# A Hymba block on one core: half blocks of matmuls between the transposes of the norm stretch, two more tiles' first products there, and the last phase's first loads and splits issued early

## The chip, the cores and the metric

The kernel runs on one core of a Trainium2 chip. The metric is the time of one execution on the device in microseconds (us). Five engines run their own instruction streams and wait for each other by semaphores: TensorE (PE in the rows), VectorE (DVE), ScalarE (ACT), GpSimd (POOL) and SyncE (SP), which here issues all DMAs.

## What is computed

One decoder block over 1,024 tokens (and 16 meta tokens), width 1,024, feed-forward width 2,816, everything in float32. The part that matters here:

```python
h = h + rms_norm(mix @ w_out, ln_post_mix)       # post_norm
hn = rms_norm(h, ln_pre_ffn)                     # second_norm
gu = hn @ w_gate_up
ff = (silu(gu[..., :D_FF]) * gu[..., D_FF:]) @ w_down
h = h + rms_norm(ff, ln_post_ffn)
```

## The kernel before

A float32 product runs as three matmuls on a high and a low part of each operand (high·high, high·low, low·high). The high part is a rounding copy (ACT, a CAST row), the low part the difference (DVE); the code calls making them a split. Times below are those of the profiled execution.

**Attention and projections** end at about 525 us. The change leaves the order of all engines there as it is.

**The norm stretch** (525 to 617 us). For each of the eight row tiles (128 tokens) the rest of the out-projection is added to `y` (half blocks `pz`, 12 matmuls each, `half_out`), `post_norm` scales it (a factor `ry` made by ACT and POOL, a gain multiply `y<-y,gpost` on POOL, the residual add on DVE), `second_norm` multiplies by the second norm's factor `rh` and the gain `gfb` (one DVE instruction), and the result is transposed on TensorE through `ident` into a PSUM tile (`tz`, `tzt`; two buffers) from which ACT and DVE split it into the operands `b11`, `b21` (tiles 0 to 3), `b22` and the sums `bt1` to `bt4` (tiles 4 to 7). The sums' inputs `c` come from `combine_rows` (three POOL and one DVE instruction per tile).

**The main loop** (617 to 1025 us) takes 22 tiles of the feed-forward width. Each is a Strassen–Winograd scheme of seven products of 12 matmuls (128x512) with DVE, ACT and POOL work beside. Products 1 and 2 of a tile ("11"·b11 and "12"·b21) need only the first half of the norms, so `blocks` runs those of the first `N_AHEAD` = 3 tiles inside the stretch, into PSUM banks `q`. The other operands of a tile are sums of weight blocks: `combos` (four POOL instructions `cw`), each then split into `as`. After each product `after` reads its bank: an ACT copy (`s<-q`, `p<-q`), a DVE add, a Silu on ACT. Every second tile POOL forms activation sums (`store_acts`, four instructions `s<-s`) and, but for the last, sums of down-projection weights (`store_down`, four `rd`), which SP stores to DRAM (`act`, `down`).

**The last phase** (1025 to about 1243 us) is the down projection in 77 steps of 12 matmuls. Each step loads one `act` block and one weight block back (`rab`), splits both into `hl`, and multiplies into eight banks (`px`, `py`). The splits of the last 11 steps are made ahead, from step 33 on, one in every three steps.

**Order.** PE, ACT, DVE and POOL are pinned to the order in which the code issues their instructions up to the end of the main loop; SP and the last phase are ordered by a scheduler. In the code before, that scheduler also moved loads and splits of the last phase's first steps up into the last tiles of the main loop.

Of the kernel before, what the change touches and what calls it, by code (L numbers as in the profile page):

```python
# [21 lines left out]
P = 128  # L22
# [75 lines left out]
def hymba_kernel(ctx, tc, x, meta, rel_bias, g_pre_mix, g_post_mix, g_pre_ffn, g_post_ffn,  # L98
# [4 lines left out]
    class Pinned:  # L103
# [49 lines left out]
    ident = cp.tile([P, P], F32, name="ident")  # L153
    make_identity(nc, ident)
# [3 lines left out]
    bfb = cp.tile([P, 8], F32, name="bfb")  # L158
    mix71 = cp.tile([P, 2, 512], F32R, name="mix71")
    pool.memset(cp.tile([P, PAD_LEFT], F32, name="pad_left"), 0.0)  # L160
# [798 lines left out]
    def down(dst, acts, ws_, t, half):  # L959
# [3 lines left out]
        for i, ((ah, al), (wh, wl)) in enumerate(zip(acts, ws_)):  # L963
            pe.matmul(dst, ah[:, ts_], wh[:, hs], start=i == 0, stop=False)
            pe.matmul(dst, ah[:, ts_], wl[:, hs], start=False, stop=False)
            pe.matmul(dst, al[:, ts_], wh[:, hs], start=False, stop=i == n - 1)

# [174 lines left out]
    t3l = h2p.tile([P, 4, HALF], F32R, name="bt3l")  # L1142
    bp, b_st = open_pool("bst", "left")
    psB_st = ExitStack()
    psB = psB_st.enter_context(tc.tile_pool(name="psB", bufs=1, space=PSUM, reuse_waits="tile"))

    def half_out(t, half):
        g = psB.tile([P, 512], F32, name=f"pz{t}{half}", tag="G", bufs=6)
        down(g, mh, wos_b, t - 4, half)
        ys = y_of[t][:, half * 512:half * 512 + 512]  # L1150
        return lambda: dve.tensor_tensor(ys, g, ys, op=ALU.add)
# [7 lines left out]

    gfb = bp.tile([P, D], F32, name="gfb")  # L1160
    sp.dma_start(gfb, g_pre_ffn[0].partition_broadcast(P))
# [8 lines left out]
    def combine_rows(t):  # L1170
# [3 lines left out]
        pool.tensor_tensor(t3, b22, b12, op=ALU.subtract)  # L1174
        pool.tensor_tensor(t1, b12, b11, op=ALU.subtract)
        pool.tensor_tensor(t2, t3, b11, op=ALU.add)
        rows_of[t] = dict(zip(("t3", "t1", "t2", "t4"), c))
        return lambda: dve.tensor_tensor(t4, b21, t2, op=ALU.subtract)
# [3 lines left out]
    def transposes(src, n, t):  # L1182
# [4 lines left out]
        split(tp, b_op[n][0][:, :, cs], b_op[n][1][:, :, cs])  # L1187


    op_homes = iter("gggg" + "ww" + "wwggg" + "oooog" + "wwwwo" + ("ggggooo" + "wwwwooo") * NF)  # L1190

    def op_tile(name):
        home = next(op_homes)
        pl, tag = (gup, "gu") if home == "g" else (ws, "whl") if home == "w" else (opp, "op")
# [50 lines left out]
    def product(dst, f_, an, bn, fresh, last):  # L1245
        (bh, bl), a = b_op[bn], a_op.pop((f_, an))
        for k in range(4):
# [357 lines left out]
```

## Time and profile before

| what | value |
|---|---|
| runs | 1254.54, 1255.61, 1252.38 us; median 1254.54 |
| the profiled execution's own time, and its span | 1251.34 us, 1249.5 us |
| mean granted clock of TensorE in it | 0.972 |
| TensorE busy | 1174.8 us (94% of the span) |
| DVE, ACT, POOL busy | 775.5, 554.2, 524.9 us |
| out-projection ends, norm stretch | 525 to 617.10 us |
| main loop, 148 products | 617.10 to 1025.42 us |

A profile row gives the start, the duration, the engine, the operation, out<-in by the program's names, how many instructions run together (x), and in brackets how long the engine had been idle just before and which engine's result ended that. The granted clock is 1.00 at 2.4 GHz and 0.50 at 1.2 GHz; a value between is a mixture over the slice.

### The profile page before, as it was taken

The numbers are of one execution on the slowest core, as the hardware profiler recorded it, in microseconds if no ns is written. First come the engines' busy times: TensorE is split into PE (matmuls) and PEld (weight loads), VectorE is DVE, ScalarE is ACT, GpSimd is POOL, SyncE is SP. The second block draws the span as 40 slices with busy tenths as digits, with TensorE's granted clock in tenths as the row PEclk, the third lists the DMA queues.
The fourth block names the chain that finished last, engine by engine and source line by source line (L and its number), as shares of the span: only waits on it lengthen the run. The fifth ranks groups of instructions, "written<-read, shape, count | busy, mean of one in ns | idle before, by whom it ended". The sixth has DMA issues, their size and how long they took to land.

```text
span 1249.5 us, 17350 instructions
## 1 busy us (share of the span) xinstructions
PE 1174.8 (94%) x5967; PEld 997.5 (80%) x5967; DVE 775.5 (62%) x1625; ACT 554.2 (44%) x1178; POOL 524.9 (42%) x529
## 2 busy tenths in 40 slices
PE   7989999999999899876799999999999999999997
PEld 6978889988988787764688888888888777888876
DVE  6477776656666777576566555555556634446764
ACT  5366565555554543342533333333333324445541
POOL 7243234343433333376357557665567630000001
PEclk9999999999999999977899999999999999999999
DMA  7521123131311512532235455435455358666745
GB/s 225 155 76 41 38 66 99 44 92 45 91 44 45 155 44 76 184 119 67 68 104 193 150 177 177 156 132 166 146 186 182 133 202 266 186 198 223 252 154 200
DMA packets 133383, 167.31 MB, mean 134 GB/s; under 512 B 10612, under 2 KB 82292, under 8 KB 133294
## 3 DMA queue, kind: packets, MB, share of 16 engines
q1 hardware_dynamic: 133294, 166.20, 41.8%
q8 instruction: 47, 0.77, 0.3%
q14 instruction: 42, 0.34, 0.1%
HBM read 114.17 MB, written 46.56 MB: 129 GB/s over the span
## 4 chain that ended last, share of the span: by engine, by line
PE 72%; DVE 8%; POOL 6%; DMA 5%; issue 5%; ACT 3%; SPq 0%; POOLq 0%; DVEq 0%; ACTq 0%
PE q L113 30%; PE px L113 7%; PE py L113 5%; PE pvb L113 3%; PE pk L113 3%; PE pqb L113 3%; PE of L113 3%; PE pqa L113 2%; PE sf L113 2%; DMA rab<-act 2%; PE tf L113 2%; PE pyb L113 2%; PE pya L113 1%; PE o L113 1%; DVE hl L113 1%
## 5 line engine op out<-in xcount | busy, mean ns | idle before, releaser
L113 DVE TENSOR_TENSOR hl<-rab,hl 128x512 fp32r<-128x512 f32 x154 | 101.8, 707 | 84.3 <-ACT hl L113 84.0
L113 DVE TENSOR_TENSOR as<-cw,as 128x512 fp32r<-128x512 f32 x88 | 89.1, 1014 | 72.5 <-ACT as L113 71.7
L113 ACT CAST hl<-rab 128x512 fp32r<-128x512 f32 x154 | 87.9, 619 | 91.1 <-DMA rab<-act 37.2
L113 PE MATMUL px<-hl,hl 128*128 128x512 f32 x528 | 122.2, 393 | 2.7 <-ACT hl L113 2.7
L113 PEld LDWEIGHTS px<-hl,hl 128*128 128x128 f32 x528 | 100.0, 190 | 24.3 <-ACT hl L113 3.1
L113 PE MATMUL py<-hl,hl 128*128 128x512 f32 x396 | 90.5, 389 | 2.6 <-DVE hl L113 2.6
L113 PEld LDWEIGHTS py<-hl,hl 128*128 128x128 f32 x396 | 74.2, 188 | 18.4 <-DVE hl L113 3.0
L113 POOL TENSOR_TENSOR s<-s,s 128x512 f32<-128x512 f32 x44 | 69.3, 1596 | 32.1 <-DVE s L113 31.2
L113 POOL TENSOR_TENSOR cw<-wgu 128x512 f32<-128x512 f32 x22 | 29.9, 1359 | 124.0 <-DMA wgu<-in_w_gate_up_dram 85.3
L113 POOL TENSOR_SCALAR PF<-PF,lf 128x144 f32<-128x144 f32 (+3 forms) x64 | 51.4, 804 | 63.9 <-DVE lf L113 48.1
L113 POOL TENSOR_SCALAR rf0v<-sa 128x1 f32<-128x1 f32 x1 | 0.6, 562 | 180.8 <-DVE sa L113 180.8
L113 ACT ACTIVATE s<-s 128x512 f32<-128x512 f32 x44 | 27.8, 632 | 109.4 <-DVE s L113 109.4
L113 DVE TENSOR_TENSOR s<-q,s 128x512 f32<-128x512 f32 x66 | 45.5, 689 | 44.1 <-PE q L113 40.3
L113 ACT ACTIVATE PF<-PF,nf 128x144 f32<-128x144 f32 (+3 forms) x64 | 50.5, 790 | 47.2 <-DVE nf L113 46.4
L113 POOL TENSOR_TENSOR rd<-rd 128x512 f32<-128x512 f32 x44 | 65.4, 1486 | 12.3 <-DMA h<-h_dram 9.7
L113 ACT COPY s<-q 128x512 f32<-128x512 f32 x44 | 25.9, 588 | 95.6 <-PE q L113 65.5
L113 DVE TENSOR_TENSOR a<-wgg,a 128x512 fp32r<-128x512 f32 x44 | 47.7, 1089 | 31.7 <-ACT a L113 31.7
L113 PE MATMUL q<-b11h,a 128*128 128x512 f32 x176 | 62.2, 416 | 3.1 <-ACT b11h L113 3.1
L113 ACT CAST as<-cw 128x512 fp32r<-128x512 f32 x88 | 54.2, 618 | 20.8 <-PE q L113 15.8
L113 PE MATMUL q<-bt4h,a 128*128 128x512 f32 x176 | 59.1, 397 | 3.8 <-DVE p L113 3.8
L113 POOL TENSOR_SCALAR P<-P,ls 128x272 f32<-128x272 f32 (+1 forms) x64 | 29.6, 483 | 77.1 <-DVE ls L113 63.2
L113 PE MATMUL q<-b21h,a 128*128 128x512 f32 x176 | 60.9, 408 | 0.0
(468 smaller groups left out, 3407.4 us busy)
## 6 DMA issues: line engine op xcount, KB each, us to landing
act<-s SPq DMA_DIRECT2D x77, 256.0 KB, 3.7
rab<-act SPq DMA_DIRECT2D x77, 256.0 KB, 2.9
wgg<-in_w_gate_up_dram SPq DMA_DIRECT2D x25, 512.0 KB, 4.3
wgu<-in_w_gate_up_dram SPq DMA_DIRECT2D x22, 512.0 KB, 3.9
rd<-in_w_down_dram SPq DMA_DIRECT2D x11, 1024.0 KB, 4.9
down<-rd SPq DMA_DIRECT2D x44, 256.0 KB, 2.2
rab<-down SPq DMA_DIRECT2D x44, 256.0 KB, 3.6
wi<-in_w_in_dram SPq DMA_DIRECT2D x18, 512.0 KB, 3.7
```

The source lines that it names most:

```text
L113: i = fn(*a, **k)
```

## The change

The diff, cut to what changes the order of work or adds to it:

```diff
+            if i % 2 and i < n - 1:
+                yield
...
+    snp, snap_st = open_pool("snap", "left")
     bp, b_st = open_pool("bst", "left")
+    gfb = bp.tile([P, D], F32, name="gfb")
+    sp.dma_start(gfb, g_pre_ffn[0].partition_broadcast(P))
...
-        down(g, mh, wos_b, t - 4, half)
+        yield from down_parts(g, mh, wos_b, t - 4, half)
...
-    gfb = bp.tile([P, D], F32, name="gfb")
-    sp.dma_start(gfb, g_pre_ffn[0].partition_broadcast(P))
...
-        split(tp, b_op[n][0][:, :, cs], b_op[n][1][:, :, cs])
...
+        hi, lo = [x[:, :, cs] for x in b_op[n]]
+        act.copy(hi, tp)
+        between()
+        dve.tensor_tensor(lo, tp, f(hi), op=ALU.subtract)
...
-    N_AHEAD = 3
+
+    N_AHEAD, SNAP = 5, (3, 4)
+    p1_of, early_of = {}, {}
+
+    def first_products(f_):
+        for i, (an, bn) in ((1, ("11", "11")), (3, ("12", "21"))):
+            banks[f_, i] = b = bank(f"q{i}_{f_}")
+            for part in range(2):
+                product(b, f_, an, bn, True, i == 3, part)
+                if part == 0:
+                    yield None
+            if f_ not in SNAP:
+                yield lambda: None
+            elif i == 1:
+                both = snp.tile([P, 2, HALF], F32, name=f"early{f_}")
+                p1_of[f_], early_of[f_] = both[:, 0], both[:, 1]
+                yield lambda f_=f_, b=b: act.copy(p1_of[f_], b)
+            else:
+                yield lambda f_=f_, b=b: dve.tensor_tensor(early_of[f_], b, p1_of[f_], op=ALU.add)
...
-                yield half_out(t, half)
-        for f_ in range(N_AHEAD):
-            for i, (an, bn) in ((1, ("11", "11")), (3, ("12", "21"))):
-                banks[f_, i] = bank(f"q{i}_{f_}")
-                product(banks[f_, i], f_, an, bn, True, i == 3)
-                yield lambda: None
+                yield from half_out(t, half)
+        for f_ in SNAP + tuple(f_ for f_ in range(N_AHEAD) if f_ not in SNAP):
+            yield from first_products(f_)
 
     work = blocks()
-    add = [lambda: None]
-
-    def unit():
-
-        last = add[0]
-        add[0] = next(work, None) or (lambda: None)
-        return last
+    follow = []
+
+    def unit(n=1):
+
+        for _ in range(n):
+            got = next(work, None)
+            for x in follow:
+                x()
+            follow[:] = [got] if got else []
...
-    preps = {0: prepare_gate(0, act), 1: prepare_gate(1, act)}
-    for n in range(10):
-        if 1 <= n < 7:
+    preps = {0: 3, 1: 4, 4: 0, 5: 1, 6: 2}
+    for n in range(4):
+        gate = prepare_gate(preps[n], act) if n in preps else None
+        if n:
             square_sum(n + 1, "rh", junk[0])
-        first = unit() if n < 4 else None
-        if n < NT:
-            second_norm(n)
-        if first:
-            first()
-        if 5 <= n < 9:
-            fourth = combine_rows(n - 1)
+        unit(2)
+        second_norm(n)
+        if n:
+            transposes(halves(n - 1)[0], "11", n - 1)
+        unit()
+        if n:
+            transposes(halves(n - 1)[1], "21", n - 1)
+        unit()
+        post_norm(n + 2)
+        first_sum(n + 3)
+        if gate:
+            run(gate)
...
         if n >= 6:
-            transposes(rows_of[n - 2]["t3"], "t3", n - 2)
-            transposes(rows_of[n - 2]["t1"], "t1", n - 2)
-        if 1 <= n < 5:
-            transposes(halves(n - 1)[0], "11", n - 1)
-            transposes(halves(n - 1)[1], "21", n - 1)
-        elif 5 <= n < 9:
+            late = rows_of[n - 2]
+            transposes(late["t3"], "t3", n - 2, third[n - 2])
+        if n < NT:
+            second_norm(n)
+        if 5 <= n < 9:
+            first, second, third[n - 1] = combine_rows(n - 1)
+            first()
+        if n == 4:
+            transposes(halves(3)[0], "11", 3)
+        unit()
+        if n >= 6:
+            transposes(late["t1"], "t1", n - 2, (lambda: post_norm(n + 2)) if n + 2 < NT else lambda: None)
+        elif n == 5:
+            transposes(halves(4)[1], "22", 4, lambda: post_norm(7))
+        else:
+            post_norm(6)
+        unit()
+        if n == 4:
+            transposes(halves(3)[1], "21", 3)
+        elif 6 <= n < 9:
             transposes(halves(n - 1)[1], "22", n - 1)
-        if n < 9:
-            second = unit()
-        if n + 2 < NT:
-            post_norm(n + 2)
-        second()
-        second = lambda: None
-        if n >= 6:
-            transposes(rows_of[n - 2]["t2"], "t2", n - 2)
-            transposes(rows_of[n - 2]["t4"], "t4", n - 2)
         first_sum(n + 3)
         if 5 <= n < 9:
-            fourth()
-        if n in preps:
-            run(preps[n])
-        if n == 2:
-            for c in combos(0, bp, 2):
-                c()
-        elif n == 3:
-            preps[4] = prepare_gate(2, act)
-        elif n == 7:
-            split_block(0, "s1")
-        elif n == 8:
-            split_block(0, "s2")
-            split_block(0, "s4")
-    run(work)
-    for n in ("s3", "22"):
-        split_block(0, n)
+            second()
+        unit()
+        if n >= 6:
+            transposes(late["t2"], "t2", n - 2)
+        if n >= 7:
+            unit()
+        if n >= 6:
+            transposes(late["t4"], "t4", n - 2)
+        if gate:
+            run(gate)
+    unit(20)
...
+    pending = combos(0, fp, 2)
...
+        def read(to, b):
+            if p1 is None:
+                act.copy(to, b)
+            else:
+                dve.tensor_tensor(to, b, p1, op=ALU.add)
...
-            act.copy(p5_of[f_], b2)
+            read(p5_of[f_], b2)
...
-            act.copy(s_tile(f_, 1), b1)
+            read(s_tile(f_, 1), b1)
...
+            if p1 is not None:
+                dve.tensor_tensor(p1, b1, p1, op=ALU.add)
+            dve.tensor_tensor(s_of[f_, 0], b1 if p1 is None else p1, s_of[f_, 0], op=ALU.mult)
...
+        if n == 6 and f_ in SNAP:
+            banks[f_, 1], fresh = bank(f"q4_{f_}"), True
...
     held = None
+    names = ("s1", "s2", "s4", "s3", "22")
+    first, second = pending
+    first()
+    split_block(0, "s1")
+    second()
+    for n in names[1:]:
+        split_block(0, n)
     for f_ in range(N_AHEAD):
-        after(f_, 1)
-        after(f_, 2)
+        if f_ in SNAP:
+            s_of[f_, 0] = early_of[f_]
+            act.activation(early_of[f_], early_of[f_], AF.Silu)
+        else:
+            after(f_, 1)
+            after(f_, 2)
...
-        steps = []
+        parts = [lambda: [load(n) for n in range(3)]] + [lambda: None] + [lambda n=n: split_step(n) for n in range(3)]
...
-    sp.dma_start(gpost2, g_post_ffn[0].partition_broadcast(P))
...
-                load_h1(t)
+                if t == 3:
+                    load_h1(t)
...
     LOAD, SPLIT = 6, 3
-    done_load = done_split = 0
+    done_load = done_split = 3
...
-        if steps[n][0] >= 3 and n % 3 == 0 and early < len(steps):
+        if n == 4:
+            sp.dma_start(gpost2, g_post_ffn[0].partition_broadcast(P))
+        if n in (7, 18, 29):
+            load_h1((n - 7) // 11)
+        if n >= NP and n % 5 == 0 and early < len(steps):
             load(early)
             split_step(early)
             early += 1
```

In words: `down` and `product` can now run in two halves of six matmuls, and `unit()` sets one half (or one block) between two transposes. `N_AHEAD` is 5; tiles 3 and 4 go first, their first two products are copied (ACT) and added (DVE) into SBUF (`early`), and later reads add that part (DVE) where an ACT copy stood; product 6 of these tiles gets a bank of its own, `q4`. The gain `gfb` is loaded ahead of the rows `xt`. `combos(0)` and all splits of tile 0's sums come after the last transpose. Not shown: operand tiles get other buffers (`mix71` serves as one of them), the sums in `store_acts` have two buffers instead of four and each is stored as soon as it is made, and the last phase's step list, `load` and `split_step` move up unchanged but for which of two buffers they take.

Three places in the order of the engines. First TensorE in the middle of the stretch, before: `q1_1` is the first product of tile 1, `tz` and `tzt` are sets of four transposes, `c2_4` the second sum of row tile 4.

```order
L113 MATMUL q1_1_6941<-b11h_6542,a11_1_6678 128x512
L113 MATMUL tzt24_6954<-ident_63,c2_4_6871 128x128 x4
L113 MATMUL tzt44_6961<-ident_63,c4_4_6872 128x128 x4
L113 MATMUL tzt35_6977<-ident_63,c3_5_6906 128x128 x4
L113 MATMUL tzt15_6984<-ident_63,c1_5_6907 128x128 x4
L113 MATMUL tz226_6991<-ident_63,y6_5343 128x128 x4
L113 MATMUL q3_1_6998<-b21h_6544,a12_1_6681 128x512
```

After, where the first product of tile 0 stands at this place:

```order
L113 MATMUL q1_0_6975<-b11l_6543,a11_0_6858 128x512
L113 MATMUL q1_0_6975<-b11h_6542,a11_0_6858 128x512
L113 MATMUL tzt24_6983<-ident_70,c2_4_6875 128x128 x4
L113 MATMUL tzt44_6990<-ident_70,c4_4_6876 128x128 x4
L113 MATMUL tzt35_7003<-ident_70,c3_5_6940 128x128 x4
L113 MATMUL q1_0_6975<-b11h_6542,a11_0_6858 128x512
L113 MATMUL q1_0_6975<-b11l_6543,a11_0_6858 128x512
L113 MATMUL q1_0_6975<-b11h_6542,a11_0_6858 128x512 x2
L113 MATMUL q1_0_6975<-b11l_6543,a11_0_6858 128x512
L113 MATMUL q1_0_6975<-b11h_6542,a11_0_6858 128x512
L113 MATMUL tzt15_7024<-ident_70,c1_5_6941 128x128 x4
```

A product now stands in two halves with transposes between; six sets of transposes had stood almost back to back.

Second, the end of the stretch. On POOL the four `cw0` rows of `combos(0)` stood inside the stretch before, ahead of the factors of row tiles 4 and 6:

```order
L113 TENSOR_TENSOR y5_5342<-y5_5342,gpost_5905 128x1024
L113 TENSOR_TENSOR cw00_6746<-wgu0_6744 128x512
L113 TENSOR_TENSOR cw00_6746<-cw00_6746,wgg0_6742 128x512
L113 TENSOR_TENSOR cw01_6747<-wgg0_6742,wgu0_6744 128x512
L113 TENSOR_TENSOR cw01_6747<-wgg0_6742,cw00_6746 128x512
L113 TENSOR_SCALAR rh4v_6754<-srh4_6752 128x1
L113 TENSOR_TENSOR rh4r_6755<-rh4v_6754,mhalf_68 128x1
```

After, they stand behind the last sums of row tile 7:

```order
L113 TENSOR_TENSOR c2_6_7014<-c3_6_7012,y2_5339 128x512
L113 TENSOR_TENSOR c3_7_7081<-y7_5344 128x512
L113 TENSOR_TENSOR c1_7_7082<-y7_5344,y3_5340 128x512
L113 TENSOR_TENSOR c2_7_7083<-c3_7_7081,y3_5340 128x512
L113 TENSOR_TENSOR cw00_7199<-wgu0_7197 128x512
L113 TENSOR_TENSOR cw00_7199<-cw00_7199,wgg0_7195 128x512
L113 TENSOR_TENSOR cw01_7200<-wgg0_7195,wgu0_7197 128x512
```

On ACT, before, from the splits of the last transposes on (`a22_0` is tile 0's last weight block, `s00` its first read of a bank):

```order
L113 CAST bt2h_6913<-tzt27_7105 128x4x128
L113 CAST bt4h_6915<-tzt47_7112 128x4x128
L113 CAST as3_0_7132<-cw01_6747 128x512
L113 CAST a22_0_7135<-wgu0_6744 128x512
L113 COPY s00_7146<-q1_0_6833 128x512
L113 ACT_TABLE_LOAD
L113 ACTIVATE s00_7146<-s00_7146 128x512
L113 COPY s10_7150<-q1_1_6941 128x512
L113 ACTIVATE s10_7150<-s10_7150 128x512
L113 COPY s20_7154<-q1_2_7057 128x512
L113 ACTIVATE s20_7154<-s20_7154 128x512
L113 CAST as1_1_7179<-cw10_7162 128x512
```

After, from the same splits of tile 0's sums on:

```order
L113 CAST as3_0_7217<-cw01_7200 128x512
L113 CAST a22_0_7220<-wgu0_7197 128x512
L113 COPY s00_7223<-q1_0_6975 128x512
L113 ACT_TABLE_LOAD
L113 ACTIVATE s00_7223<-s00_7223 128x512
L113 COPY s10_7227<-q1_1_7059 128x512
L113 ACTIVATE s10_7227<-s10_7227 128x512
L113 COPY s20_7231<-q1_2_7128 128x512
L113 ACTIVATE s20_7231<-s20_7231 128x512
L113 ACTIVATE early3_6835<-early3_6835 128x512
L113 ACTIVATE early4_6909<-early4_6909 128x512
L113 CAST as1_1_7258<-cw10_7241 128x512
```

All splits of tile 0's sums moved behind the last transposes (`as1_0`, `as2_0`, `as4_0` stand in the three rows above this piece), and two activations of `early` are new ahead of `as1_1`.

Third, DVE in the last tile but one of the main loop. Before, with the splits `hl` of the last phase's first steps in it:

```order
L113 TENSOR_TENSOR a11_21_9922<-wgg21_9901,a11_21_9922 128x512
L113 TENSOR_TENSOR as1_21_9942<-cw210_9905,as1_21_9942 128x512
L113 TENSOR_TENSOR hl00_10238<-rab0_10217,hl00_10238 128x512
L113 TENSOR_TENSOR as2_21_9959<-cw210_9905,as2_21_9959 128x512
L113 TENSOR_TENSOR hl01_10241<-rab0_10217,hl01_10241 128x512
L113 TENSOR_TENSOR a12_21_9977<-wgg21_9901,a12_21_9977 128x512
L113 TENSOR_TENSOR s200_9925<-q3_20_9964,s200_9925 128x512
L113 TENSOR_TENSOR as3_21_9994<-cw211_9906,as3_21_9994 128x512
L113 TENSOR_TENSOR hl10_10244<-rab1_10220,hl10_10244 128x512
L113 TENSOR_TENSOR p5_20_9945<-q1_20_9907,p5_20_9945 128x512
L113 TENSOR_TENSOR as4_21_10010<-cw211_9906,as4_21_10010 128x512
L113 TENSOR_TENSOR hl11_10247<-rab1_10220,hl11_10247 128x512
```

After, the splits come behind tile 20's last multiplications:

```order
L113 TENSOR_TENSOR as2_21_9948<-cw210_9894,as2_21_9948 128x512
L113 TENSOR_TENSOR a12_21_9966<-wgg21_9890,a12_21_9966 128x512
L113 TENSOR_TENSOR s200_9914<-q3_20_9953,s200_9914 128x512
L113 TENSOR_TENSOR mix71_69<-cw211_9895,mix71_69 128x512
L113 TENSOR_TENSOR p5_20_9934<-q1_20_9896,p5_20_9934 128x512
L113 TENSOR_TENSOR as4_21_9998<-cw211_9895,as4_21_9998 128x512
L113 TENSOR_TENSOR s201_9951<-q2_20_9916,s201_9951 128x512
L113 TENSOR_TENSOR a22_21_10015<-wgu21_9892,a22_21_10015 128x512
L113 TENSOR_TENSOR s200_9914<-q1_20_9896,s200_9914 128x512
L113 TENSOR_TENSOR s201_9951<-p5_20_9934,s201_9951 128x512
L113 TENSOR_TENSOR hl00_10095<-rab0_10057,hl00_10095 128x512
L113 TENSOR_TENSOR hl01_10098<-rab0_10057,hl01_10098 128x512
```

`p5_20`, which empties the bank of tile 20's product 7, no longer stands behind `hl10`.

## Rows read from the trace of the kernel before

**Rows 1.** The page's first part: busy time of each engine, share of the span.

```profile
PE 1174.8 (94%) x5967; PEld 997.5 (80%) x5967; DVE 775.5 (62%) x1625; ACT 554.2 (44%) x1178; POOL 524.9 (42%) x529
```

**Rows 2.** Windows: PE, PEld, DVE, ACT, POOL busy; granted clock; DMA share, GB/s.

```profile
525.00:550.00 25.00, 20.05 (x89) 16.41 (x88) 19.72 (x23) 10.41 (x19) 16.72 (x14) 0.86 0.56 201
550.00:575.00 25.00, 12.91 (x48) 9.51 (x47) 15.10 (x13) 7.96 (x16) 22.90 (x20) 0.73 0.30 101
575.00:600.00 25.00, 16.06 (x67) 12.27 (x65) 13.32 (x16) 6.77 (x12) 14.14 (x12) 0.72 0.09 25
...
625.00:650.00 25.00, 25.00 (x112) 20.68 (x111) 15.25 (x18) 8.22 (x16) 11.37 (x8) 1.00 0.29 93
```

**Rows 3.** Timeline of PE in the norm stretch and at the main loop's start.

```profile
531.62 1.97 PE L113 MATMUL tz<-ident,y 128*128 128x128 f32 x8 [4.95 <-DVE y L113]
...
555.01 0.80 PE L113 MATMUL q<-b11h,a 128*128 128x512 f32 x1 [3.06 <-ACT b11h L113]
559.70 0.79 PE L113 MATMUL q<-b11l,a 128*128 128x512 f32 x1 [3.90 <-DVE b11l L113]
...
564.56 0.81 PE L113 MATMUL tz<-ident,y 128*128 128x128 f32 x4
...
572.17 1.11 PE L113 MATMUL tzt<-ident,c 128*128 128x128 f32 x4 [4.04 <-POOL c L113]
...
617.10 0.40 PE L113 MATMUL q<-bt1h,as 128*128 128x512 f32 x1
...
619.86 0.39 PE L113 MATMUL q<-bt2h,as 128*128 128x512 f32 x1
```

**Rows 4.** Timeline of SP's queue: the load of the second norm's gain.

```profile
523.30 0.48 SPq L1161 DMA_DIRECT2D gfb<-in_ln_pre_ffn_dram  x1
```

**Rows 5.** Timeline of DVE: second norms of row tiles 0 and 2.

```profile
530.28 1.28 DVE L113 SCALAR_TENSOR_TENSOR y<-y,rh0r,gfb 128x1024 f32<-128x1024 f32 x1 [9.45 <-DMA gfb<-in_ln_pre_ffn_dram]
...
540.47 3.41 DVE L113 SCALAR_TENSOR_TENSOR y<-y,rh2r,gfb 128x1024 f32<-128x1024 f32 x1
```

**Rows 6.** Timeline of POOL: gains of row tiles 2, 4 and 6, `combos(0)`, first sum of tile 4.

```profile
523.59 2.40 POOL L113 TENSOR_TENSOR y<-y,gpost 128x1024 f32<-128x1024 f32 x1
...
539.40 3.40 POOL L113 TENSOR_TENSOR y<-y,gpost 128x1024 f32<-128x1024 f32 x1
...
550.89 1.27 POOL L113 TENSOR_TENSOR cw<-wgu 128x512 f32<-128x512 f32 x1
...
555.55 1.27 POOL L113 TENSOR_TENSOR cw<-wgg,cw 128x512 f32<-128x512 f32 x1
...
559.70 2.37 POOL L113 TENSOR_TENSOR y<-y,gpost 128x1024 f32<-128x1024 f32 x1
...
570.86 1.26 POOL L113 TENSOR_TENSOR c<-y 128x512 f32<-128x512 f32 x1
```

**Rows 7.** Timeline of ACT where the norm stretch ends.

```profile
613.97 0.62 ACT L113 CAST a<-wgu 128x512 fp32r<-128x512 f32 x1
614.49 0.59 ACT L113 COPY s<-q 128x512 f32<-128x512 f32 x1
...
621.16 0.58 ACT L113 COPY p<-q 128x512 f32<-128x512 f32 x1
```

**Rows 8.** Timeline of POOL: sums of the first two tiles' activations, then of weights.

```profile
648.62 6.78 POOL L113 TENSOR_TENSOR s<-s,s 128x512 f32<-128x512 f32 x4 [3.87 <-DVE s L113]
655.36 6.40 POOL L113 TENSOR_TENSOR rd<-rd 128x512 f32<-128x512 f32 x4
```

**Rows 9.** Timeline of PE: the waits from the last tile on.

```profile
1001.95 0.79 PE L113 MATMUL q<-bt4h,a 128*128 128x512 f32 x1 [3.79 <-DVE p L113]
...
1006.36 0.39 PE L113 MATMUL q<-b11h,a 128*128 128x512 f32 x1
...
1036.45 23.44 PE L113 MATMUL px<-hl,hl 128*128 128x512 f32 x96 [2.70 <-ACT hl L113]
...
1190.80 21.84 PE L113 MATMUL py<-hl,hl 128*128 128x512 f32 x95 [2.61 <-DVE hl L113]
```

More of the change, by code (lines that the diff above doesn't have):

```diff
@@ L957, in load_rows, with down_parts @@
         return hi, lo
-    def down(dst, acts, ws_, t, half):
+    def down_parts(dst, acts, ws_, t, half):
         n = len(acts)
@@ L1243, in split_block, with product @@
         split_op(f_, n, blocks_of[f_][n])
-    def product(dst, f_, an, bn, fresh, last):
-        (bh, bl), a = b_op[bn], a_op.pop((f_, an))
-        for k in range(4):
+    def product(dst, f_, an, bn, fresh, last, part=None):
+        (bh, bl), a = b_op[bn], a_op[f_, an]
+        for k in range(4) if part is None else range(2 * part, 2 * part + 2):
             pe.matmul(dst, a[:, 0, k], bh[:, k], start=fresh and k == 0, stop=False, skip_group_check=True)
@@ L1381, in combined @@
     def combined(name, tag, op, a, b):
-        r = fp.tile([P, HALF], F32, name=name, tag=tag, bufs=4)
+        r = fp.tile([P, HALF], F32, name=name, tag=tag, bufs=2)
         pool.tensor_tensor(r, a, b, op=op)
@@ L1491, in split_step @@
             parts_of[n].append(hl)
+    held = None
+    names = ("s1", "s2", "s4", "s3", "22")
[5 more added lines that the diff above has]
+        split_block(0, n)
+    for f_ in range(N_AHEAD):
+        if f_ in SNAP:
[4 more added lines that the diff above has]
+            after(f_, 2)
+    pending = combos(1, fp, 2)
+    for f_ in range(NF):
+        ahead = f_ < N_AHEAD
+        order = (5, 6, 3, 7, 4) if ahead else (1, 5, 6, 2, 7, 3, 4)
+        names = ("s1", "s2", "s4", "s3", "22") if f_ + 1 < N_AHEAD else ("11", "s1", "s2", "12", "s3", "s4", "22")
+        parts = [lambda: [load(n) for n in range(3)]] + [lambda: None] + [lambda n=n: split_step(n) for n in range(3)]
+        if f_ + 1 < NF:
+            first, second = pending
+            parts = [lambda n=n: split_block(f_ + 1, n) for n in names]
+            if len(order) < len(names):
+                s2, s3 = parts[1:3], parts[3:5]
+                parts = [parts[0], lambda: [c() for c in s2], lambda: [c() for c in s3]] + parts[5:]
+            s0, s1 = parts[0:2]
+            parts[0] = lambda: (first(), s0())
+            parts[1] = lambda: (second(), s1())
+        parts = iter(parts)
+        for i, n in enumerate(order):
+            if n == 4 and ahead:
+                held = f_
+                next(parts, lambda: None)()
+                continue
+            multiply(f_, n, next(parts, lambda: None))
+            if i == 0 and held is not None and held != f_:
+                multiply(held, 4)
+                held = None
+        if f_ + 2 < NF:
+            pending = combos(f_ + 2, fp, 2)
+        j = f_ - 1
+        if j > 0 and j % 2:
+            store_acts(j // 2)
+            store_down(j // 2)
@@ new lines, in hymba_kernel @@
+    store_down(NP - 1)
+    store_acts(NP - 1)
+    pinned.difference_update(("pe", "act", "dve", "pool"))
+    op_st.close()
+    snap_st.close()
+    h2_st.close()
+    f_st.close()
+    wa_st.close()
+    psB_st.close()
+    psC = ctx.enter_context(tc.tile_pool(name="psC", bufs=1, space=PSUM, reuse_waits="tile"))
+    rows, rows_st = open_pool("rows", "left")
+    last, last_st = open_pool("last", "left")
+    sp_, s_st = open_pool("stage", "right")
+    y = [rows.tile([P, D], F32, name=f"ff{t}") for t in range(NT)]
@@ L1493, in products @@
+    gpost2 = rows.tile([P, D], F32, name="gpost2")
+    X = [psC.tile([P, HALF], F32, name=f"px{i}", tag="X0" if i < 2 else "X1", bufs=2) for i in range(2)]
+    Y = [psC.tile([P, HALF], F32, name=f"py{i}", tag="Y", bufs=4) for i in range(4)]
+    X += [psC.tile([P, HALF], F32, name=f"px{i}", tag="X1", bufs=2) for i in range(2, 4)]
     def products(n, tiles):
```

115 lines of the change are left out of this document (42 added, 73 removed).

## The prediction

> **What bounds the kernel now.** The busy shares come first: TensorE works 1174.8 of 1249.5 us [rows 1], so it idles 74.7 us in all, and no other engine is near its limit as a mean. The windows then show where: in the main loop every slice is like 625 to 650 us, TensorE busy without a gap at full granted clock, while from 525 to 600 us it idles 4.95 + 12.09 + 8.94 = 26.0 us and the clock granted is 0.86, 0.73 and 0.72 [rows 2]. The reader should see two losses in one stretch there: waits, and matmuls at a mixture of the two levels. A product of 12 matmuls takes 619.86 - 617.10 = 2.76 us at full clock, in the mean of the main loop (1025.42 - 617.10 - 5.5 of waits) / 148 = 2.72, and 564.56 - 559.70 = 4.86 us after a wait [rows 3].
>
> The timeline of TensorE names the waits one by one [rows 3]: on DVE's `y`, on splits of `b11`, on POOL's sum `c`. The start of that chain stands on DVE and SP: DVE idles 9.45 us for the gain `gfb` [rows 5], which SP issued only at 523.30 [rows 4], so that it landed 6.9 us later. Behind that, POOL sets the pace: gain multiplies at 539.40 and 559.70, `combos(0)` from 550.89 to 556.8 between them, and the first sum `c` at 570.86 [rows 6]. Three waits remain outside the stretch, of 3.79, 2.70 and 2.61 us [rows 9].
>
> **Stretch, early part.** `gfb` is now issued ahead of the rows, where SP issues its first `xt` rows, about 514.9 by the position of the load in the queue (an estimate), and lands by 521.8 with the same 6.9 us. The next limit is POOL's multiply for row tile 2, which ends at 523.59 + 2.40 = 526.0 [rows 6]; its DVE add stood behind the second norm that waited until 530.28 + 1.2. So the chain of norms gains 5.5 us, not the whole 9.45. `combos(0)` leaves POOL's stream there: 6.0 us more for row tiles 4 to 7, of which part is lost to waits on TensorE. I put the first `c` at 562 instead of 570.86.
>
> **Stretch, TensorE.** The first `q` product can begin at 555.01 - 5.5 - about 1 for the pair of transposes it no longer follows = 548.5; I let it and the next run at 4.86 and 3.9 us with a wait of 2 us between, then one at full rate, so that the first `tzt` starts at 563.3 (572.17 before, with two products done instead of three). From there TensorE has 7 products x 2.72 = 19.0 us and 18 sets of transposes up to the last but one. A set takes 0.81 us at the low level [rows 3], half of that at the full, so 7.3 to 8 us; I add 1.5 us for waits. That sets T0, the end of the set that reads row tile 7's second sum, at 563.3 + 19.0 + 8 + 1.5 = 592. A half block takes 1.36 us, half of 2.72, and the split of a set some 1.3 (0.62 for a cast of 512 columns [rows 7] and 0.64 on DVE, half of the 1.28 for 1,024 [rows 5]), so each hides one. The low bound is 588, without any wait. All at the low level it is 7 x 2.14 + 18 x 0.4 + the product before = 25 us later, 617. I take 592: in the same trace the half blocks `pz` with transposes between ran at full clock once the waits ahead of them were over.
>
> **The new wait at the end of the stretch.** In the old order tile 0's sums were ready and product 5 followed the last product of the stretch without a gap at 617.10 [rows 3]. Now POOL starts them only at T0, because their buffers are those of the stretch. Four `cw` take 5.3 us at 1.27 each with starts between [rows 6]. The first makes `as1` ready 2.9 us after T0 (1.27, a cast, a difference). ACT runs the casts in the order s1, s2, s4, s3, 22, the s4 cast not before the last sum, and only then the copy `s00` that empties the bank product 6 writes: it starts about T0 + 7.1. From that copy's start to the end of the copy `p` of product 5's bank took 621.16 + 0.58 - 614.49 = 7.25 us [rows 7]; two new Silu stand in it, 0.54 each by the 0.52 from one start to the next at 613.97 [rows 7]. So product 3, which needs that bank, waits until T0 + 15.4. At full rate products 5 and 6 would end at T0 + 0.4 + 5.4 and product 3 start there: 9.6 us lost, and 1.6 us because a product after a wait runs partly at the lower level (1006.36 - 1001.95 = 4.41 for 2.72 [rows 9]): 11.2 us. Bounds: 6, if ACT's chain loses the waits that lie inside the 7.25, to 14, if every product there runs like the one at 1001.95.
>
> **Main loop.** Four products move out: 10.9 us. The 144 left take 391.7. The wait of 3.79 us is gone with its slow product (1.7): 5.5 us, since DVE's read of the bank no longer stands behind splits that waited for loads [rows 9]. The other splits of the first three steps lie beside products in tile 21, whose DVE is free half of the time. New: tile 3 keeps five products (13.6 us), and POOL's 6.78 + 6.40 us of sums fall into it [rows 8] as before, when seven products gave more time; DVE's read of tile 3's product 5 then stands behind a split that POOL makes late. I count 4 us (0 to 5). The sum: T0 592 + 0.4 + 11.2 + 391.7 + 4 = 999.3, against 1025.42 at the same place: 26.1 us less.
>
> **Last phase.** The fourth step's weight load no longer queues behind the last stores, so of the 2.70 us wait and the slow start after it I take 2.0 (half of the wait to 3). The early splits, spread from step 15 on, lift the burst at the 2.61 us wait: 1.5 (0 to 2.9) [rows 9]. The other moves (order of stores, buffers, `gpost`, `h1`) put transfers beside others that the trace shows with room, and I cost them at nothing; if they collide, a wait of some 3 us like these returns.
>
> **Sum.** 26.1 + 2.0 + 1.5 = 29.6 us. The profiled execution's own time, 1251.34, becomes 1221.7; the median lies 3.2 above it, so I forecast 1225.
>
> **A rule against the trace.** DVE's instruction with two inputs took 3.41 us at 540.47 beside a POOL multiply of 3.40 [rows 5, 6], where the usual durations are 1.28 and 2.40. The Trainium skill, SBUF — State Buffer, section "SBUF: two separate sides", states that in this pairing the two share an exclusive lock on a port pair, held for the whole instruction. At the new wait POOL's four sums would then alternate with DVE's differences (0.68 us each), which makes that wait some 2 us longer and the forecast 1227. The trace agrees in kind; I keep 1225, because DVE is nearly idle there otherwise.
>
> **Rivals.** (a) More gain: the sums and copies at T0 overlap as far as the bounds allow, T0 is 588, tile 3 does not wait: 4 + 5 + 4 + 1 less, 1211. The short `cw` rows speak for it; the order on ACT against it.
> (b) Less gain: norms, not TensorE, still set the pace; POOL's busy share of 22.90 in 25 us at 550 [rows 2] and DVE instructions of double length beside it [rows 5] speak for that. T0 is 602: 1235.
> (c) No gain: TensorE stays at 1.2 GHz up to T0, because short waits recur between half blocks: 25 us later, 1250. The granted clock of 0.73 and 0.72 [rows 2] speaks for it, the gaps that go speak against it. The Trainium skill, TensorE: Matmul & The Clock Gate, section "HAM oscillation — how this bites in real kernels", describes a kernel in which waits between groups of matmuls bring the low level back each time; no run here shows it yet for half blocks.
> (d) Slower: half blocks ahead of transposes fill nothing, because the engine is in order and each half block waits for its own operand; the stretch then takes the 617.10 - 555.01 = 62.1 us from the first product as before, plus four products at 4.86: 548.5 + 62.1 + 19.4 = 630, 38 us behind my T0: 1263. It decides from a T0 past 625 on. That the sums `c` wait for buffers freed by transposes speaks for it; that the products' operands are ready long before from row tile 4 on speaks against it.
>
> **How the numbers follow.** My forecast 0.58, (a) 0.17, (b) 0.13, (c) 0.06, (d) 0.06. A measurement of this kernel can tell about 0.3% from no change, 1250.8 to 1258.3 on the median. All of the forecast, (a) and (b) is faster, 0.88, and half of (c) as well, less 0.03 for mishaps not listed: 0.88; same 0.05, slower 0.07. For 8 in 10 the range takes the forecast with its bounds, most of (a) and most of (b): 1209 to 1242.
>
> **What would show it.** Right: DVE's multiply by `gfb` near 521 without a wait on a DMA; the first `q` product near 548; the last transposes near 592; behind them TensorE idle for some 2, 2 and 5 us, released by `as`, `s` and `p`; no wait of 3.79 us in the last tiles; the main loop's end near 999. Wrong: granted clock below 0.8 from 555 to 592, or waits on `c` or `bt` of more than 2 us each between the half blocks, which would be (c) or (d); no gap after the last transposes, which would be (a).

## The result, and the profile after

The changed kernel takes 1226.08 us (median; 1225.12 to 1227.29) against 1254.8 us before: ratio 0.9775, 95% interval 0.9758 to 0.9792, 28.7 us less. The two profiled executions differ by less: their spans are 1249.5 and 1224.9 us, 24.6 us apart, because that of before lies 3.5 us below its kernel's median and that of after 0.7 us above. The steps below go by the spans.

The windows after, with the columns of [rows 2]:

```profile
525.00:550.00 25.00, 18.11 (x92) 14.29 (x90) 24.51 (x24) 11.77 (x23) 17.29 (x19) 0.95 0.58 201
550.00:575.00 25.00, 19.08 (x82) 13.80 (x83) 19.53 (x20) 10.91 (x21) 21.01 (x17) 0.92 0.36 120
575.00:600.00 25.00, 21.90 (x123) 17.96 (x123) 16.30 (x22) 9.22 (x17) 10.39 (x8) 1.00 0.21 64
600.00:625.00 25.00, 18.83 (x63) 14.05 (x64) 13.00 (x16) 12.88 (x23) 14.51 (x11) 0.80 0.22 64
```

From 550 to 600 us TensorE is busy 41.0 us where it was 29.0, and the granted clock is 0.92 and 1.00 instead of 0.73 and 0.72. The slice behind, where the main loop starts, now has the lowest clock: 6.2 us idle, clock 0.80. Those are the new waits. From 525 to 550 us TensorE idles 6.9 us where it was 4.95: the half blocks `pz` end 7.3 us earlier there (543.8), the first `q` product comes only 4.5 us earlier. The timeline of TensorE shows all three (the counterpart of [rows 3]):

```profile
546.41 0.66 PE L113 MATMUL tz<-ident,y 128*128 128x128 f32 x4 [2.58 <-DVE b11l L113]
550.51 0.80 PE L113 MATMUL q<-b11h,a 128*128 128x512 f32 x1 [3.44 <-ACT b11h L113]
...
564.28 0.66 PE L113 MATMUL tzt<-ident,c 128*128 128x128 f32 x4 [1.09 <-POOL c L113]
...
570.07 0.66 PE L113 MATMUL tz<-ident,y 128*128 128x128 f32 x4 [1.50 <-DVE bt3l L113]
...
572.89 1.16 PE L113 MATMUL tzt<-ident,c 128*128 128x128 f32 x8 [0.78 <-DVE bt1l L113]
575.01 0.63 PE L113 MATMUL tzt<-ident,c 128*128 128x128 f32 x4 [0.96 <-DVE bt2l L113]
...
580.34 0.66 PE L113 MATMUL tz<-ident,y 128*128 128x128 f32 x4 [1.47 <-DVE bt3l L113]
...
597.27 1.04 PE L113 MATMUL tzt<-ident,c 128*128 128x128 f32 x8
599.93 0.50 PE L113 MATMUL q<-bt1h,as 128*128 128x512 f32 x1 [1.61 <-ACT as L113]
...
606.18 0.50 PE L113 MATMUL q<-bt2h,as 128*128 128x512 f32 x1 [0.98 <-ACT s L113]
...
613.87 0.79 PE L113 MATMUL q<-b22h,as 128*128 128x512 f32 x1 [4.67 <-ACT p L113]
```

The row at 597.27 holds the last sums' transposes. Behind it product 5 waits for a cast, product 6 for the copy of its bank, product 3 for the copy of product 5's bank. POOL's first sum `c`, and POOL and ACT behind the last transposes (two timelines):

```profile
562.28 1.94 POOL L113 TENSOR_TENSOR c<-y 128x512 f32<-128x512 f32 x1
...
597.96 1.26 POOL L113 TENSOR_TENSOR cw<-wgu 128x512 f32<-128x512 f32 x1 [10.20 <-PE tzt L113]
...
602.23 1.72 POOL L113 TENSOR_TENSOR cw<-wgg,cw 128x512 f32<-128x512 f32 x1
```

```profile
603.98 1.14 ACT L113 CAST as<-cw 128x512 fp32r<-128x512 f32 x2 [2.76 <-POOL cw L113]
605.03 0.61 ACT L113 CAST a<-wgu 128x512 fp32r<-128x512 f32 x1
605.55 0.58 ACT L113 COPY s<-q 128x512 f32<-128x512 f32 x1
...
611.70 1.13 ACT L113 ACTIVATE early<-early 128x512 f32<-128x512 f32 x2
...
613.25 0.57 ACT L113 COPY p<-q 128x512 f32<-128x512 f32 x1
```

The start of the chain, on DVE (the counterpart of [rows 5]): the gain is there, and the next limit is POOL's multiply of row tile 2.

```profile
520.16 1.28 DVE L113 SCALAR_TENSOR_TENSOR y<-y,rh0r,gfb 128x1024 f32<-128x1024 f32 x1
...
525.43 1.29 DVE L113 SCALAR_TENSOR_TENSOR y<-y,ry2r,xt 128x1024 f32<-128x1024 f32 x1 [3.39 <-POOL y L113]
...
533.00 3.31 DVE L113 SCALAR_TENSOR_TENSOR y<-y,ry3r,xt 128x1024 f32<-128x1024 f32 x1
```

The late waits (the counterpart of [rows 9]): none is left in the last tiles or in the third quarter of the last phase; tile 3 has a new one.

```profile
658.38 0.47 PE L113 MATMUL q<-b22h,as 128*128 128x512 f32 x1 [1.03 <-DVE p L113]
...
1005.72 8.32 PE L113 MATMUL px<-hl,hl 128*128 128x512 f32 x36
1015.43 0.50 PE L113 MATMUL px<-hl,hl 128*128 128x512 f32 x1 [1.39 <-ACT hl L113]
```

### The profile page after: what moved, and what is told of

The parts are those of the page before. It is cut to its first block, busy times and chain, and to the rows that moved or that the text cites. A ratio compares the mean times of both kernels' runs of the same rounds, so it can differ in the third digit from the quotient of the medians.

```text
span 1224.9 us, 17388 instructions
## 1 busy us (share of the span) xinstructions
PE 1164.0 (95%) x5967; PEld 987.7 (81%) x5967; DVE 786.0 (64%) x1631; ACT 551.8 (45%) x1174; POOL 519.7 (42%) x529
## 4 chain that ended last, share of the span: by engine, by line
PE 73%; DVE 9%; POOL 6%; issue 5%; ACT 3%; DMA 3%; SPq 0%; POOLq 0%; DVEq 0%; ACTq 0%
PE q L113 25%; PE px L113 9%; PE py L113 7%; PE pvb L113 3%; PE pqb L113 3%; PE pk L113 3%; PE of L113 3%; PE pqa L113 2%; PE sf L113 2%; PE tf L113 2%; DVE y L113 2%; PE pyb L113 2%; POOL s L113 1%; POOL cw L113 1%; PE pya L113 1%
## 5 line engine op out<-in xcount | busy, mean ns | idle before, releaser
L113 DVE TENSOR_TENSOR as<-cw,as 128x512 fp32r<-128x512 f32 x78 | 78.3, 1006 | 68.6 <-ACT as L113 67.7
L113 PEld LDWEIGHTS py<-hl,hl 128*128 128x128 f32 x396 | 74.4, 188 | 15.4
L113 POOL TENSOR_TENSOR s<-s,s 128x512 f32<-128x512 f32 x41 | 61.4, 1510 | 31.0 <-DVE s L113 27.0
L113 ACT ACTIVATE PF<-PF,nf 128x144 f32<-128x144 f32 (+3 forms) x64 | 50.5, 790 | 47.5 <-DVE nf L113 46.7
L113 DVE TENSOR_TENSOR s<-q,s 128x512 f32<-128x512 f32 x62 | 42.7, 689 | 38.1 <-PE q L113 34.3
L113 ACT CAST as<-cw 128x512 fp32r<-128x512 f32 x78 | 48.1, 618 | 33.6 <-POOL cw L113 22.6
L113 ACT COPY s<-q 128x512 f32<-128x512 f32 x40 | 23.4, 586 | 84.7 <-PE q L113 62.3
L113 PE MATMUL q<-bt1h,as 128*128 128x512 f32 x176 | 59.1, 398 | 2.1 <-ACT as L113 1.6
```

The source lines that it names most:

```text
L113: i = fn(*a, **k)
```

## The experiments

Each is the changed kernel with the edit shown; ratios are to the kernel before on the same chip. The profiled executions start the stretch at different times (the first `q` product from 549.4 to 552.5 us among those whose edit lies behind it), so the table measures stages from the first `q` product: to the start of the set that holds row tile 7's second sum, and to the end of the main loop; then the last phase (its start to the end of the span). Two profiles of the same kernel, the changed one and e9, differ by up to 1.3 us in these stages.

| kernel | ratio (95% interval) | first `q` at | to last sums | to loop end | last phase |
|---|---|---|---|---|---|
| before | 1 | 555.0 | 56.7 | 470.4 | 224.1 |
| changed | 0.9775 (0.9758 to 0.9792) | 550.5 | 46.8 | 455.2 | 219.2 |
| e1 gain late | 0.9817 (0.9792 to 0.9842) | 556.6 | 47.9 | 455.5 | 219.2 |
| e2 few matmuls | 0.9750 (0.9719 to 0.9781) | 552.1 | 43.8 | 451.9 | 220.1 |
| e3 whole blocks | 0.9794 (0.9770 to 0.9818) | 552.4 | 50.4 | 458.9 | 218.6 |
| e4 late splits old | 0.9848 (0.9822 to 0.9874) | 551.3 | 46.9 | 463.5 | 220.3 |
| e5 reads first | 0.9730 (0.9702 to 0.9757) | 551.4 | 46.7 | 451.5 | 218.9 |
| e6 gates later | 0.9761 (0.9740 to 0.9781) | 550.6 | 48.1 | 455.7 | 218.4 |
| e7 three ahead | 0.9743 (0.9719 to 0.9768) | 550.4 | 39.8 | 454.9 | 219.9 |
| e8 spacing old | 0.9821 (0.9795 to 0.9847) | 552.5 | 46.7 | 455.0 | 223.4 |
| e9 changed again | 0.9771 (0.9739 to 0.9803) | 549.7 | 48.1 | 455.6 | 220.3 |
| e10 three, late sums | 0.9743 (0.9711 to 0.9774) | 548.1 | 39.2 | 452.6 | 218.8 |
| e11 five, reads first | 0.9760 (0.9726 to 0.9794) | 549.4 | 47.6 | 453.0 | 219.2 |
| e12 three, reads first | 0.9728 (0.9697 to 0.9759) | 550.3 | 43.2 | 450.8 | 219.0 |

One thousandth of the ratio is 1.25 us.

**e1.** `sp.dma_start(gfb, ...)` goes back behind the six `xt` loads.

> The changed kernel with one part undone: the gain gfb is loaded behind the six row loads again. T0 is the end of the set of transposes that reads row tile 7's second sum (597.7 us in the changed kernel). Theory: the chain of norms starts 5.5 us later and carries that up to T0, so T0 near 603 and the time near 1231 (5 us more). Rival: POOL and ACT set the pace later anyway and absorb it, T0 within 1 us of 597.7 and the time within 1.5 us of the changed kernel's 1226.

Measured: ratio 0.0042 higher, 5.3 us (the intervals just touch). The first `q` product comes at 556.6, later than in all other changed kernels (548.1 to 552.5), and the stages behind it are as long as in the changed kernel and e9. In its trace DVE waits 9.86 us for the gain again, up to 531.31. The theory holds: the chain carries the delay to the end, and the early load is worth some 5 us.

**e2.** It leaves out 10 of 12 matmuls of four products:

```diff
-                product(b, f_, an, bn, True, i == 3, part)
+                if f_ in SNAP:
+                    (bh, bl), a = b_op[bn], a_op[f_, an]
+                    pe.matmul(b, a[:, 0, part], bh[:, part], start=part == 0, stop=part == 1, skip_group_check=True)
+                else:
+                    product(b, f_, an, bn, True, i == 3, part)
```

> The changed kernel with work left out: of each of the four first products of tiles 3 and 4 only 2 of 12 matmuls run, all copies and adds stay. Theory: three of the four lie ahead of the first sums' transposes, which wait for POOL's first sum anyway, so only the fourth counts: T0 2 to 3 us earlier (595), time near 1223. Rival: TensorE is the bound of the whole stretch from the first of them on, 4 x 10/12 x 2.72 = 9.1 us: T0 near 588.6, time near 1217.

Measured: 3.0 us less up to the last sums, 3 us by the ratio (the intervals overlap), as the theory said. As the granted clock fell too (last section), the price of the products may be somewhat higher. Where the products were, TensorE now waits for POOL's first sum, and at the low level:

```profile
562.63 1.12 PE L113 MATMUL tzt<-ident,c 128*128 128x128 f32 x4 [4.83 <-POOL c L113]
```

**e3.** Whole blocks; the second half's slot stays empty:

```diff
-            if i % 2 and i < n - 1:
+            if False:
                 yield
...
                 product(b, f_, an, bn, True, i == 3, part)
-                if part == 0:
-                    yield None
+            yield None
```

> The changed kernel with whole blocks of 12 matmuls where two halves stood: the first slot takes the whole block, the second none, so that transposes stand in pairs. Theory: the two PSUM buffers make the pairs wait for the split of the pair before, about 1 us at each of some nine places and a lower clock behind them: T0 near 606, time 8 to 12 us more, near 1236. Rival: the gain of the stretch comes from the earlier gain load and POOL's freed 6 us alone: T0 within 2 us of 597.7, time within 2 us of 1226.

Measured: 3.6 us more up to the last sums (2.3 more than in e9) and 2.4 us by the ratio, whose intervals overlap. Half blocks help by the traces, at a third of the price that I had put on them. With whole blocks the stretch still takes 50.4 us up to the last sums where it took 56.7 before, so most of its gain has another source.

**e4.** The first three steps' loads and splits are the scheduler's again:

```diff
-        parts = [lambda: [load(n) for n in range(3)]] + [lambda: None] + [lambda n=n: split_step(n) for n in range(3)]
+        parts = []
...
-    done_load = done_split = 3
+    done_load = done_split = 0
```

> The changed kernel with the loads and splits of the last phase's first three steps ordered by the scheduler again. Theory: DVE's read of tile 20's product 7 stands behind those splits again, a wait of 3 to 4 us and a slow product return in the last tile (5.5 us), and the wait at the fourth step grows from 1.4 towards 2.7: time 6 to 7 us more, near 1233. Rival: the stores that are now issued one by one free SP's queue, so the splits come in time: within 2 us of 1226.

Measured: 8.3 us more in the main loop, 9.2 by the ratio, where 6 to 7 were expected. The wait at the fourth step of the last phase stays at 1.49 us, so that part of the theory fails: the early splits aren't what halved it. The wait in the main loop is back, longer than before the change:

```profile
990.52 0.80 PE L113 MATMUL q<-bt4h,a 128*128 128x512 f32 x1 [5.45 <-DVE p L113]
```

**e5.** ACT's order behind the stretch (the rest of the splits and reads follows product 5's copy):

```diff
     first()
+    after(0, 1)
     split_block(0, "s1")
     second()
-    for n in names[1:]:
-        split_block(0, n)
+    split_block(0, "s2")
+    after(0, 2)
+    after(1, 1)
+    after(1, 2)
+    split_block(0, "s4")
```

> The changed kernel with another order on ACT behind the last transposes: the reads of tile 0's and tile 1's banks and their Silu stand between the casts of s1, s2 and s4, the copy of product 5's bank comes right after it, and s3, 22, tile 2's reads and the two early Silu behind that. Theory: the long wait there (product 3 starts 16.6 us after the last sum set begins, 10 us late) is the length of ACT's chain, not POOL's sums; product 3 then starts about 9 us after T0 and the time falls by 7 us, near 1219. Rival: POOL's sums and the next tile's weight load, which lands about 10 us after T0, are the real bound, so that the wait only moves to product 5 of tile 1: 3 us or less, 1223 or more.

Measured: 3.7 us less up to the loop's end, 5.6 by the ratio. The waits at products 6 and 3 are gone, one of 2.96 us stands at product 7, and tile 3's is 2.59 instead of 1.03. Both theories had a part: ACT's order made the waits at products 6 and 3, and some 2 of the 5.6 us came back in other places.

**e6.** `run(gate)` for tiles 0 to 2 stands one round later.

> The changed kernel with the splits of the weight blocks of tiles 0, 1 and 2 placed one round later in the stretch, behind the splits of row tiles' transposes instead of ahead of them on DVE. Theory: the waits of 1.50, 0.78, 0.96 and 1.47 us between 570 and 580 us come from DVE's queue, in which two such splits (2.4 to 2.6 us a pair) stand ahead of the difference that frees the transposes' buffer: 2 to 3 us less up to T0, time near 1223.5. Rival: they come from the two buffers and POOL's sums themselves: within 0.7 us of the changed kernel.

Measured: the waits at 570 and 580 shrink, one of 2.90 us appears between, and the last sums come no earlier. The theory falls: this order gains nothing. It doesn't clear the splits, for the wait went where they went. A pair of them now stands at 571.64 on DVE, for 2.35 us, ahead of the split `bt2l` that the new wait is for:

```profile
575.33 1.09 PE L113 MATMUL tzt<-ident,c 128*128 128x128 f32 x4 [2.90 <-DVE bt2l L113]
```

**e7.** Three tiles ahead and `combos(0)` in the stretch (operand tiles in the buffers of before):

```diff
-    N_AHEAD, SNAP = 5, (3, 4)
+    N_AHEAD, SNAP = 3, ()
...
+        if n == 2:
+            for c in combos(0, bp, 2):
+                c()
```

> The changed kernel without the two more tiles: three tiles ahead, nothing parked, and with the memory that this frees, combos(0) inside the stretch again; half blocks, gain load and last phase stay. Theory: four products return to the main loop (10.9 us), T0 comes 6 to 9 us earlier because only 3 us of them were paid there and fewer blocks are left at its end, and the wait behind T0 shrinks from 12 to about 5 us: about even, 1220 to 1230, so that the parked products bought next to nothing net. Rival: the parked products are a main source of the gain: 1234 or more.

Measured: 0.9743, no slower than the changed kernel, and the last sums come 7.0 us earlier, as the theory said. Four products more in the main loop cost nothing net.

**e8.** Last phase: old places of the early splits, the gain and the residual rows.

> The changed kernel with the last phase's ahead-of-time splits, the last gain and the residual rows in their old places (from step 33 on, one in three steps). Theory: the burst of splits on DVE and ACT from there makes TensorE wait once for some 2.6 us in the third quarter, with a slow start behind it: 3 to 4 us more, near 1229.5. Rival: the wait was due to the order of loads before and doesn't return: within 1 us of 1226.

Measured: 3.1 to 4.2 us more in the last phase than in the changed kernel's two profiles, 5.8 by the ratio. The edit moves three things at once. The old wait for a split is back, and the one at the fourth step stays small (1.04 us):

```profile
1170.90 23.19 PE L113 MATMUL py<-hl,hl 128*128 128x512 f32 x95 [2.51 <-DVE hl L113]
```

**e9.** No edit.

> The changed kernel itself, as the yardstick of the three others on the same chip. Every theory: ratio to the kernel before within 0.976 to 0.979, the same waits behind T0 (1.6, 0.5, 1.0 and 4.7 us).

Measured: as expected, but for the waits at products 6 and 3, 2.46 and 3.10 us: 5.6 in sum as in the first profile.

**e10.** e7's first edit alone; `combos(0)` stays behind the transposes.

> The changed kernel without the two more tiles, but with combos(0) behind the last transposes as in the change: it tells the parked products from the place of combos(0). Theory: the parked products do pay by themselves (10.9 us less in the main loop for about 3 in the stretch), and it was the late sums, for which they took the memory, that ate it: this kernel is 5 to 8 us slower than the changed one and 6 to 10 slower than three ahead with the sums in the stretch. Rival: the parked products pay nothing even so: within 2 us of the changed kernel.

Measured: 1223.75 us against 1226.66 for the changed kernel on the same chip. The theory falls: the parked products pay nothing even with the late sums. The last sums come 7.6 us earlier, product 3 9.7 us earlier after the first `q` product, and no wait follows in tile 3:

```profile
587.26 1.94 PE L113 MATMUL tzt<-ident,c 128*128 128x128 f32 x8 [1.05 <-DVE bt3l L113]
590.40 0.79 PE L113 MATMUL q<-bt1h,as 128*128 128x512 f32 x1 [1.19 <-ACT as L113]
...
601.77 0.50 PE L113 MATMUL q<-b22h,as 128*128 128x512 f32 x1 [2.96 <-ACT p L113]
```

**e11.** e5, and product 6's copy ahead of the next tile's casts.

> The changed kernel with ACT's order behind the last transposes as in the run with reads first, and in addition the copy of product 6's bank ahead of the next tile's casts, which wait for a weight load. Theory: the wait of 2.96 us at product 7 goes too, and the kernel is 6 to 9 us faster than the changed one (ratio near 0.971). Rival: the wait moves on to the next tile's product 5, whose first sum comes with the load: 3 to 5 us faster, as with the first order.

Measured: 2.6 us less up to the loop's end than in e9, 1.4 by the ratio, within its uncertainty. Neither theory nor rival came: the wait of 2.67 us stays at product 7, and tile 3's is 2.60. On ACT the copy that product 7 waits for, at 611.87, still stands behind tile 2's reads and the two early Silu, and there ACT had waited 2.06 us for DVE.

**e12.** e7 with `combos(0)` split in the stretch as before the change, and e11's order of reads.

> Three tiles ahead, nothing parked, combos(0) and its first splits inside the stretch as before the change, and the reads of the banks early on ACT behind it; half blocks, gain load and last phase as changed. Theory: hardly any wait is left behind T0, so it is 5 to 8 us faster than three ahead without this order and the fastest of all, ratio near 0.969. Rival: DVE, which then has the splits again between the transposes, makes T0 later by as much: no faster than three ahead, ratio 0.974.

Measured: 1221.42 us (1220.5 to 1224.32) against 1226.66 (1225.54 to 1230.31) for the changed kernel on the same chip. The runs of the two don't overlap, the intervals of their ratios do. In its trace product 5 is released by the last transposes' split, and no wait follows up to the last phase:

```profile
595.94 0.79 PE L113 MATMUL q<-bt1h,as 128*128 128x512 f32 x1 [0.55 <-DVE bt2l L113]
```

It has the lowest median, and 4.8 us less than e9 up to the loop's end agrees with its time; from e5 (0.9730) it can't be told. Against e7 it gains 1.9 us by the ratio, not 5 to 8: of the waits behind T0 only one of 0.55 us is left, but the last sums come 43.2 us after the first `q` product instead of 39.8, so the rival had most of it.

## Why the prediction was right

The direction, the size (28.7 us on the medians for 29.6) and the places were right; on the spans 24.6 us came, so that the closeness to 1225 is luck in part: the main loop ended at 1005.7 for a forecast of 999.3, 6.4 us late, the last phase won 1.4 more than forecast, and 4.1 of the 28.7 us are the distances of the two profiled executions to their medians. Two slips in the working changed little: the row at 559.70 holds 11 matmuls, so that 4.86 us is the time of 11 and not of 12, and without any wait the terms give 563.3 + 19.0 + 7.3 = 589.6, not the low bound of 588. Step by step:

**Early part.** The second norm of row tile 0 began at 520.16 without a wait for the gain, and POOL's multiply was the next limit at 525.43 for a forecast of 526.0. The first sum `c` came at 562.28 for 562, the first `tzt` at 564.28 for 563.3. The first `q` product came at 550.51 for 548.5, behind waits of 2.58 us for a split `b11l` and 3.44 us for a cast `b11h`. e1 confirms the load as the cause.

**T0.** Forecast 592, measured 597.7, the end of the first four transposes in the row at 597.27. From 564.28 on it took 33.4 us instead of 28.7. The term that was mis-sized is "I add 1.5 us for waits": it was 4.9 us (0.20, 1.50, 0.78, 0.96, 1.47), which is 3.4 of the 4.7 us. In e6 another place for the weight splits didn't shorten the stage. That DVE instructions which take longer beside POOL make these waits is argued from rows, not shown by a run: the two weight splits ahead of the wait at 570 took 2.38 us and DVE's norm row behind it 2.21, where 1.28 is the usual time of either (see the last section).

**The new wait.** Forecast behind T0: product 5 after 2.9, the copy `s00` at 7.1, product 3 at 15.4. Measured: 2.2, 7.85 and 16.2 us. Mechanism and size were right, and e5 and e11 show that ACT's order is what makes it long, since the waits at products 6 and 3 go with it, but for 0.54 us in e11. They also show that this isn't free: a wait of 2.7 to 3.0 us comes up at product 7, and tile 3's grows by 1.6 us.

**The rule on the shared port pair** in the Trainium skill, SBUF — State Buffer, section "SBUF: two separate sides", would have made that wait 2 us longer. The four sums took 602.23 + 1.72 - 597.96 = 6.0 us instead of 5.3: the trace agrees in kind with a third of the price. Two of tile 0's differences on DVE fell beside them, and only the two sums that began behind such a difference took longer, 1.74 us (at 600.53) and 1.72, where the others took 1.26 and 1.27.

**Main loop and last phase.** No wait of 3.79 us is left; e4 shows that the early splits did it, and prices them at 8 to 9 us in this kernel, since without them it would wait longer than the old one; against the kernel before they remove the wait and the slow product behind it, 5.5 us. Tile 3 waited 1.03 + 0.53 us, and tile 4 0.56, for a forecast of 4 with bounds 0 to 5. The last phase gained 4.9 us (3.8 in e9's profile) for 3.5, and e8 puts 3.1 to 4.2 of it on the spacing with the gain and the residual rows. The wait at the fourth step fell from 2.70 to 1.39 us; e4 and e8 leave it low, and the order of the stores, which the forecast named for it, was not undone in any run.

**Rivals.** (a) did not come: T0 was later than forecast, and tile 3 waited. (c) did not come: the granted clock rose to 0.92 and 1.00. (d) did not come: T0 lay far below 625. (b) is half true: T0 lies midway between the forecast and its 602, by the waits of 4.9 us.

**What the sum hid.** "Four products move out: 10.9 us" is right for the main loop alone. e10 shows the whole account: the last sums 7.6 us later, product 3 2.1 later on top (9.7 in all), and tile 3's waits. TensorE's gap ahead of the first sums holds three products, and it is nearly full with three tiles as well (a wait of 1.88 us for `c` is left in e10); e2 takes most of four products out, three of them in that gap, and wins only 3 us. The products beyond are paid again, by e10 in full. So the parts that have a price are the gain load (5 us), the early splits of the last phase (8 to 9), the spacing (3 to 6) and the half blocks (2 to 4). These are prices in the changed kernel, each taken alone; they need not add up to the gain over the kernel before, where the early splits stand for 5.5. With that figure they are 15.5 to 20.5 of the 24.6 us on the spans.

The rest is not shown. POOL's freed 6 us can hardly be it, going by the two kernels with three tiles: in e10, where `combos(0)` is out of POOL's stream, the first `tzt` comes 14.6 us after the first `q` product instead of 16.7 in e7, but the last sums after 39.2 instead of 39.8. Product 3 then comes 1.9 us later than in e7, and e7 has a wait of 2.75 us in its last tile that e10 lacks, so the two end alike by the ratio. What no run undoes is the new order of the rounds on DVE, ACT and POOL (where `post_norm`, the parts of `combine_rows` and the weight splits stand between the transposes). It is the untested candidate for what e3 leaves of the stretch's gain.

## What to carry to other kernels

Moving work into a stretch that waits pays only up to the width of the waits ahead of the step that sets its pace: count which of the moved instructions stand before that step, and price the others in full. A load that one early instruction needs, when a chain starts there, is worth its delay up to the next limit: here 5 of the 9.45 us that DVE had waited. When work leaves a stretch for lack of memory, look at the order of work on the engines behind it: here the order of ACT's casts and copies, more than the sums, made the new wait, and part of what another order freed was lost again further on.

## What was not expected of the hardware

DVE's 128x1024 instruction of a norm, 1.27 to 1.29 us in nine of the fourteen cases from 520 us on, took 2.21 to 3.31 us in five (3.31 at 533.00, shown above). Each of the five began while a 128x512 or 128x1024 instruction of POOL was running, and each ended 1.08 us after that one's end: as if the later one had stood still until then. Where DVE's began first, it was POOL's that took longer, 3.03 us instead of 2.40 at 549.12. The 3.41 us at 540.47 before the change fits too: 540.47 + 3.41 is 1.08 us behind the end of POOL's multiply, 539.40 + 3.40 [rows 5, 6]. In these rows the longer time follows from which of the two began first.

```profile
532.84 2.39 POOL L113 TENSOR_TENSOR y<-y,gpost 128x1024 f32<-128x1024 f32 x1
...
549.12 3.03 POOL L113 TENSOR_TENSOR y<-y,gpost 128x1024 f32<-128x1024 f32 x1
...
569.79 1.27 POOL L113 TENSOR_TENSOR c<-y 128x512 f32<-128x512 f32 x1
```

```profile
548.66 1.28 DVE L113 SCALAR_TENSOR_TENSOR y<-y,rh4r,gfb 128x1024 f32<-128x1024 f32 x1
...
569.93 2.21 DVE L113 SCALAR_TENSOR_TENSOR y<-y,rh6r,gfb 128x1024 f32<-128x1024 f32 x1
```

And with few matmuls in the stretch (e2) the granted clock of 550 to 575 us fell to 0.55, yet the kernel was not slower: most of what TensorE did there was not on the path.
